# Gate logits of the last branch as seven-product block matmuls in a fp32 two-layer trunk kernel

## The chip, the cores and the metric

The kernel runs on one core of one Trainium2 chip. The metric is the device time of one execution in microseconds (us), the median of several runs. An execution under the hardware profiler gives the trace from which all rows here come; its times count from the start of its span.

The engines are TensorE (PE: matmuls and transposes, with weight loads in rows of their own, PEld), VectorE (DVE), ScalarE (ACT), GpSimd (POOL) and SyncE (SP), which issues most DMA transfers. Each engine works through its own instructions in a fixed order and waits on semaphores of the others.

## What is computed

Two layers; in each a SwiGLU FFN, a token mixer and a second FFN, each between two RMS norms and added to the residual x. x is 512 tokens by 1024.

```python
for l in range(DEPTH):
    h = rms_norm(x, norm_pre[l, 0])
    x = x + 0.5 * rms_norm(swiglu_ffn(h, ...), norm_post[l, 0])
    h = rms_norm(x, norm_pre[l, 1])
    m = hybrid_mixer(h, ...)
    x = x + rms_norm(m, norm_post[l, 1])
    ...                                   # second FFN like the first

def hybrid_mixer(h, w_in, ...):
    proj = h @ w_in                       # all inputs of the branches, and 3 x 1024 gate logits
    ...                                   # sb_out: stick-breaking attention
    ...                                   # conv_out: GLU, causal depthwise conv of 31 taps, LayerNorm, swish
    ...                                   # gla_out: gated linear attention
    branches = jnp.stack([sb_out, conv_out, gla_out], axis=2)      # each 512 wide
    branch_d = jnp.einsum('bsgw,gwd->bsgd', branches, w_branch)    # each to 1024
    gates = jax.nn.sigmoid(gate_logits.reshape(b, s, N_BRANCHES, D_MODEL))
    merged = jnp.sum(gates * branch_d, axis=2)
    return merged @ w_out
```

All of it is float32.

## The kernel before

**Products.** A float32 operand is split in two parts of a reduced float32 type: hi is a cast (ACT), lo is what is left (DVE). A product is three matmuls: hi·hi, hi·lo and lo·hi. Weights come by DMA into `raw`, are split into `whi` and `wlo` (rings of 5) and used once; `xh` and `xl` are the split, normed activations, which stay for a sub-layer.

**Gates and branches in the mixer.** The merge has 3 branches of 8 gates; a gate is 128 of the 1024 output columns. For each, PE computes the logits (`gate`, 24 matmuls of 128x512), ACT their sigmoid (`gs`), PE the branch's projection (`pb`, 12 matmuls), DVE multiplies (`gs<-pb,gs`), and POOL adds the result into `acc`. The order is attention (branch 0), gated linear attention ("GLA", branch 2), convolution (branch 1, "last"). Beside the GLA gates DVE runs the taps of the convolution and its layer norm: PE transposes `y` into `ct`, DVE makes statistics (`bs`, `mv`) and `yn`, and PE transposes `yn` back into `cb`. After the sixth GLA gate (`u_ == 5`) the last two token blocks go back; from the whole `cb` ACT makes the sigmoid `cs` and DVE the scaled `y`, then `y*cs`, then its split into `brh` and `brl`, the inputs of the last branch. PE meanwhile runs the seventh and eighth GLA gates, and then the last branch.

**Block products.** FFN tiles don't use 24 matmuls per 128 columns. `block_tiles` (L451) takes a pair of column blocks and two halves of the tokens and of the depth as a 2x2 block product with seven products in place of eight: seven times 12 matmuls of 128x256 for what plain tiling does in two times 24 of 128x512. For this it needs sums of weight blocks (`raw<-raw` on DVE), sums of token blocks `T1` to `T4` (made by the class `Forms`), and sums of the results in the PSUM banks A, B and C (copies `cp` on ACT, sums on DVE). `between(g)` is called ahead of each product g, so a caller can place other work there; weights are prepared `AHEAD` products early. The down projections (class `Down`) work with similar sums.

**What sets the order.** The instructions are written out in the order of the program text, and a scheduler at compile time fixes each engine's order from it. PE's instructions, and what is marked `pinned`, stay in program order; the rest, such as the splits of loaded weights, are placed by the scheduler. At run time each engine keeps its list. Weights are loaded through SP in the order of its list, as buffers come free.

The lines of the profile that matter: matmuls L66, transposes L71, splits L115 (ACT) and L116 (DVE), block sums, casts and wlo of `block_tiles` L455 and L457, `gs` and `acc` of the merge L1245 and L1246, the convolution's `cs`, `y` L1377 to L1379. A helper records the operations of many places, so a line can stand for several.

Of the kernel before, what the change touches and what calls it, by code (L numbers as in the profile page):

```python
# [41 lines left out]
def kernel(  # L42
# [17 lines left out]
    gp = ctx.enter_context(tc.tile_pool(name="gp", bufs=2))  # L60
    mp = ctx.enter_context(tc.tile_pool(name="mp", bufs=1))
    sm = ctx.enter_context(tc.tile_pool(name="sm", bufs=4))
    psp = ctx.enter_context(tc.tile_pool(name="psp", bufs=1, space=PSUM))

    def mm(*a, **k):
# [333 lines left out]
    class Forms:  # L399
# [7 lines left out]
        def arrive(self, i, pts):  # L407
# [11 lines left out]
            for c in range(2):  # L419
# [4 lines left out]
                for j, n in enumerate(("T3", "T4")):  # L424
                    nc.vector.tensor_tensor(self.raw[n][c][:, :, tok], t2, first[j][:, k], op=ALU.add)

        def finish(self, n):
# [20 lines left out]
    PLACES = (0, 1, 0, 2, 4, 3, 2)  # L448
    AHEAD = 6

    def block_tiles(w0, w1, fs, forms, hid, between):  # L451


        pin = pinned
        copy = lambda o, i: pin(nc.scalar.copy(o, i))  # L455
        silu = lambda o, i: pin(nc.scalar.activation(o, i, AF.Silu))
        tt = lambda o, a, b, op: pin(nc.vector.tensor_tensor(o, a, b, op=op))  # L457
        add = lambda o, a, b: tt(o, a, b, ALU.add)
        sub = lambda o, a, b: tt(o, a, b, ALU.subtract)
        n = 7 * len(fs)  # L460
        raw, banks, cps, ring = {}, {}, {}, {}

        def load(u):
            r = wp.tile([P, 5, 512], F32, tag="raw", name="raw", bufs=3)
            for w, q0 in ((w0, 0), (w1, 1)):
                for j in range(2):
                    nc.sync.dma_start(r[:, q0 + 2 * j].rearrange("p (k c) -> p k c", c=P),
                                      w[j * 512:(j + 1) * 512, fs[u] * P:(fs[u] + 1) * P]
                                      .rearrange("(k p) c -> p k c", p=P))
            raw[u] = r  # L470

        def low(g0, g1):
# [43 lines left out]

        def parts(u):
            cp = cps[u]
            return [cp[:, x * 256:(x + 1) * 256] for x in range(4)], hid[fs[u]], banks[u]

        def taken(g):

            u, j = divmod(g, 7)
            (p1, p7, u2, u4), h, (A, B, C) = parts(u)
            if j == 0:
                copy(p1, A[:, H0])
            if j == 1:
                copy(p7, C[:, H0])
            if j == 2:
                copy(u2, A[:, H0])  # L530
            if j == 4:
                copy(u4, A[:, H0])
            if j == 6:
                silu(h[:, H0], h[:, H0])
                silu(h[:, H1], A[:, H0])

        def summed(g):

            u, j = divmod(g, 7)
            (p1, p7, u2, u4), h, (A, B, C) = parts(u)  # L540
            if j == 3:
                add(h[:, H0], B[:, H0], p1)
            if j == 5:
                sub(u2, C[:, H0], u2)
                sub(u4, p7, u4)
            if j == 6:
                tt(h, cps[u][:, 512:1024], h, ALU.mult)
# [23 lines left out]
    class Down:  # L571
# [66 lines left out]
        def sums(self, p):  # L638
# [8 lines left out]
            if j >= 2:  # L647

                if self.PER == 1 and not self.apart:
                    self.apart = [gp.tile([P, D], F32, tag="g", name="kept") for n in range(2)]  # L650
# [150 lines left out]
    def ffn(wg, wu, wd, weights, forms, arrive, finish, upcoming, early, late, begin):  # L801
# [72 lines left out]
        block_tiles(wg, wu, fs, forms, hid, between)  # L874
# [4 lines left out]
    def mixer(l, wv, arrive, finish, upcoming, early, late):  # L879
# [14 lines left out]
        for i in range(NT):  # L894
# [281 lines left out]
        for h in range(HEADS):  # L1176
            ahead = att_scores(h + 1) if h + 1 < HEADS else None
            ws = att_weights(res)
            res = ahead
            if res is None:  # L1180
                for _ in fill:
                    pass
                conv_in(0)
            for _ in range(3):
                next(fill, None)
            att_values(h, ws)
        next(decay[0])
        conv_in(1)
        next(decay[0])
# [8 lines left out]

        acc = [None] * KC

        def gate_weights(g, d):
            return load_cols(W, C_GATE + g * D + d * P)

        def gate_branch(g, d, src, wb, w):
            pg = bank("gate")
            mm_cols(pg, *w)
            sg = slot("gs", tag="s")
            nc.scalar.activation(sg, pg, AF.Sigmoid)
            pb = bank("pb")
            wh, wl = wb  # L1210
# [5 lines left out]
            return pb, sg  # L1216

        def load_branch(g, d):
            wh, wl = load_cols(w_branch[l, g], d * P, 2 * P)
# [7 lines left out]
                r.append((sh, sl))  # L1227
            return r

        def gates(g, src, done):  # L1230

            early_ = done is not None
            following = gate_weights(g, 0) if early_ else None
            for d in range(0, KC, 2):
                wb = load_branch(g, d)
                for dd in (d, d + 1):
                    w = following if early_ else gate_weights(g, dd)
                    if early_ and dd + 1 < KC:
                        following = gate_weights(g, dd + 1)
                    pb, sg = gate_branch(g, dd, src, wb[dd - d], w)  # L1240
                    if acc[dd] is None:
                        acc[dd] = slot("acc", tag="q")
                        nc.vector.tensor_tensor(acc[dd], pb, sg, op=ALU.mult)
                    else:
                        nc.vector.tensor_tensor(sg, pb, sg, op=ALU.mult)  # L1245
                        nc.gpsimd.tensor_tensor(acc[dd], acc[dd], sg, op=ALU.add)  # L1246
                    if done is not None:
                        done(dd)
                    yield

        sb_gates = gates(0, branch_split(sbT, "s"), None)


        gnB = mp.tile([P, 512], F32, tag="row", name="gnB")
# [76 lines left out]
        gla_turn(*turn)  # L1331
        for _ in sb_gates:
            conv_taps(7)
        gla_gates = gates(2, branch_split(glaT, "t"), None)


        cb = []
# [44 lines left out]

        down = Down(w_out[l], acc, 0, 2, (), (4, 5, 6, 7))
        down.pairs()

        def merge(d):
            for n in range(2):
                down.sum_tokens(d, n)
            if d == KC - 2:
                for n in range(3):  # L1390
                    down.ahead()
# [23 lines left out]
    for idx, (l, s) in enumerate(subs):  # L1415
        norms = []

        def late():
            norms.append(load_g(norm_post[l, s]))
            if idx + 1 < len(subs):  # L1420
                norms.append(load_g(norm_pre[subs[idx + 1][0], subs[idx + 1][1]]))

        upcoming = []
# [58 lines left out]
```

## Time and profile before

| | |
|---|---|
| median of 3 runs | 2323.29 us (2323.27 to 2325.67) |
| profiled execution, its own time | 2321.75 us |
| its span | 2320.0 us |
| PE, DVE, ACT, POOL busy | 99%, 81%, 53%, 8% of the span |
| granted TensorE clock | 0.999 |

How to read the rows: the page's first part gives each engine's busy time, its share of the span and its count of instructions. The chain that ended last is followed back from the last instruction, and its shares say on which engine that chain lay. A row of a timeline has the start, the busy time, the engine, the line, the operation, `out<-in`, the shape and a count; in brackets stand the idle time of the engine just before it, and what ended it. Matmuls overlap in the pipeline, so the distance of two starts, not the busy time of one, is what a matmul costs. A table of stretches has one row for each stretch of time.

In layer 0 the mixer's merge lies between about 570 and 780 us, and the second layer's some 1160 us later.

### The profile page before, as it was taken

The numbers are of one execution on the slowest core, as the hardware profiler recorded it, in microseconds if no ns is written. First come the engines' busy times: TensorE is split into PE (matmuls) and PEld (weight loads), VectorE is DVE, ScalarE is ACT, GpSimd is POOL, SyncE is SP. The second block draws the span as 40 slices with busy tenths as digits, with TensorE's granted clock in tenths as the row PEclk, the third lists the DMA queues.
The fourth block names the chain that finished last, engine by engine and source line by source line (L and its number), as shares of the span: only waits on it lengthen the run. The fifth ranks groups of instructions, "written<-read, shape, count | busy, mean of one in ns | idle before, by whom it ended". The sixth has DMA issues, their size and how long they took to land.

```text
span 2320.0 us, 35537 instructions
## 1 busy us (share of the span) xinstructions
PE 2296.1 (99%) x13664; PEld 2031.0 (88%) x13664; DVE 1884.6 (81%) x2819; ACT 1240.6 (53%) x2414; POOL 177.2 (8%) x277
## 2 busy tenths in 40 slices
PE   8999999999999999999999999999999999999998
PEld 7999888887888889998889998888878888899987
DVE  7888987859965688889888889878599647888897
ACT  5555656644323565556555566566433225566664
POOL 0000001201021200000000000012010212000000
PEclk9999999999999999999999999999999999999999
DMA  5333643131333423336433336432313324333363
GB/s 174 100 101 110 229 153 102 55 103 49 110 91 106 140 73 103 99 109 235 147 87 97 108 110 235 150 88 62 97 55 105 96 91 136 91 98 104 114 222 109
DMA packets 336219, 269.49 MB, mean 116 GB/s; under 512 B 13130, under 2 KB 285548, under 8 KB 336048
## 3 DMA queue, kind: packets, MB, share of 16 engines
q1 hardware_dynamic: 336048, 267.21, 38.0%
q8 instruction: 107, 1.75, 0.3%
q14 instruction: 64, 0.52, 0.1%
HBM read 265.07 MB, written 2.10 MB: 115 GB/s over the span
## 4 chain that ended last, share of the span: by engine, by line
PE 96%; DVE 2%; ACT 1%; issue 0%; DMA 0%; POOL 0%; SPq 0%; DVEq 0%; POOLq 0%; ACTq 0%
PE A L66 19%; PE gate L66 11%; PE oA L66 10%; PE C L66 9%; PE oC L66 6%; PE pb L66 6%; PE B L66 5%; PE oB L66 3%; PE pf L66 3%; PE gr L66 2%; PE pa L66 2%; PE q L66 2%; PE gv L66 2%; PE pv L66 2%; PE pgl L66 2%; PE k L66 2%
## 5 line engine op out<-in xcount | busy, mean ns | idle before, releaser
L457 DVE TENSOR_TENSOR wlo<-raw,whi 128x1024 fp32r<-128x1024 f32 (+1 forms) x304 | 331.1, 1089 | 106.9 <-ACT whi L455 106.1
L455 ACT CAST whi<-raw 128x512 fp32r<-128x512 f32 x532 | 315.3, 620 | 164.7 <-DVE raw L457 164.7
L115 ACT CAST whi<-raw 128x1024 fp32r<-128x1024 f32 (+1 forms) x162 | 168.1, 1044 | 329.8 <-PE gate L66 143.6
L116 DVE TENSOR_TENSOR wlo<-raw,whi 128x1024 fp32r<-128x1024 f32 (+1 forms) x162 | 203.4, 1265 | 137.3 <-ACT whi L115 133.0
L457 DVE TENSOR_TENSOR raw<-raw 128x512 f32<-128x512 f32 x304 | 209.2, 688 | 5.7
L66 PE MATMUL A<-xh,whi 128*128 128x256 f32 x608 | 172.5, 284 | 0.0
L66 PE MATMUL A<-xh,wlo 128*128 128x256 f32 x608 | 172.0, 283 | 0.0
L66 PE MATMUL A<-xl,whi 128*128 128x256 f32 x608 | 172.0, 283 | 0.0
L1055 DVE SCALAR_TENSOR_TENSOR y<-u,cw,y 128x511 f32<-128x511 f32 (+14 forms) x240 | 166.7, 755 | 0.0
L686 DVE TENSOR_TENSOR wlo<-raw,whi 128x1024 fp32r<-128x1024 f32 x122 | 148.8, 1220 | 17.8 <-ACT whi L683 17.5
L683 ACT CAST whi<-raw 128x1024 fp32r<-128x1024 f32 x122 | 128.4, 1052 | 63.8 <-issue 20.8
L66 PE MATMUL gate<-xh,whi 128*128 128x512 f32 x384 | 151.3, 394 | 0.0
L66 PE MATMUL gate<-xh,wlo 128*128 128x512 f32 x384 | 149.8, 390 | 1.3 <-DVE wlo L116 1.3
L66 PE MATMUL gate<-xl,whi 128*128 128x512 f32 x384 | 149.6, 390 | 0.0
L66 PE MATMUL oA<-whi,dl 128*128 128x512 f32 x352 | 137.0, 389 | 0.0
L66 PE MATMUL oA<-whi,dh 128*128 128x512 f32 x352 | 137.0, 389 | 0.0
L66 PE MATMUL oA<-wlo,dh 128*128 128x512 f32 x352 | 136.9, 389 | 0.0
L268 POOL TENSOR_TENSOR rs<-ms,mhalf 128x1 f32<-128x1 f32 x44 | 25.1, 576 | 1415.2 <-DVE ms L266 1415.2
L455 ACT COPY cp<-A 128x256 f32<-128x256 f32 x228 | 84.4, 370 | 66.5 <-PE A L66 65.6
L66 PEld LDWEIGHTS A<-xl,whi 128*128 128x128 f32 x608 | 116.6, 192 | 0.2
L66 PEld LDWEIGHTS A<-xh,whi 128*128 128x128 f32 x608 | 116.5, 192 | 0.2
L66 PEld LDWEIGHTS A<-xh,wlo 128*128 128x128 f32 x608 | 116.5, 192 | 0.0
(330 smaller groups left out, 6947.4 us busy)
## 6 DMA issues: line engine op xcount, KB each, us to landing
raw<-in_ffn_w_down_dram SPq DMA_DIRECT2D x152, 512.0 KB, 4.5
raw<-in_w_in_dram SPq DMA_DIRECT2D x108, 512.0 KB, 4.7
raw<-in_ffn_w_gate_dram SPq DMA_DIRECT2D x168, 256.0 KB, 3.4
raw<-in_ffn_w_up_dram SPq DMA_DIRECT2D x168, 256.0 KB, 4.5
raw<-in_w_branch_dram SPq DMA_DIRECT2D x24, 512.0 KB, 4.8
raw<-in_w_out_dram SPq DMA_DIRECT2D x24, 512.0 KB, 4.9
g<-in_norm_pre_dram SPq DMA_DIRECT2D x6, 512.0 KB, 6.8
g<-in_norm_post_dram SPq DMA_DIRECT2D x6, 512.0 KB, 5.8
```

What stands on the lines that cost most here:

```text
L66: tc.keep_in_program_order(nc.tensor.matmul(*a, **k))
L115: pin(nc.scalar.copy(hi, src))
L116: pin(nc.vector.tensor_tensor(lo, src, hi.bitcast(F32), op=ALU.subtract))
L268: nc.gpsimd.tensor_tensor(self.rs, ms, mhalf[:, 0:1], op=ALU.pow)
L455: copy = lambda o, i: pin(nc.scalar.copy(o, i))
L457: tt = lambda o, a, b, op: pin(nc.vector.tensor_tensor(o, a, b, op=op))
L683: pinned(nc.scalar.copy(hi, src))
L686: pinned(nc.vector.tensor_tensor(lo, src, hi.bitcast(F32), op=ALU.subtract))
L1055: nc.vector.scalar_tensor_tensor(y[:, back:], u[:, :S - back], cw[:, c, j:j + 1], y[:, back:], op0=ALU.mult, op1=ALU.add)
```

## The change

The last branch's gate logits (branch 1, the convolution) are no longer eight times 24 matmuls of 128x512. They are made in four pairs by `block_tiles`, which takes a `source` (which columns), a `target`, a generator `result` (what is done at the end of a pair: here three sigmoids), an `ahead` (4 for this use) and a `wait`. In its `between` the mixer issues: the seventh GLA gate ahead of g = −2 and the eighth ahead of g = 0, which stood in the loop over the GLA gates; the load of the branch's weights at the third product of each pair; the branch products of the pair before, ahead of a pair's first product; the merge ahead of its second. The last pair's adds into `acc` are on DVE, the others stay on POOL.

The token sums T1 to T4 aren't there in the mixer. `Forms.rebuild` makes them from `xh` and `xl`: T1 and T2 behind the attention values of the last block (7 DVE operations and 2 casts for each half c), T3 and T4 behind the statistics of the layer norm. T1 and T2 live in the room of the residual x, which is stored to DRAM early in the mixer (`away`, four transfers of 512 KB) and loaded back during the down projection.

The convolution's layer norm begins one GLA gate earlier: the first two token blocks at `u_ == 2` (was 3), their way back and the other two at 3 (was 4). The last two still go back at `u_ == 5`.

The line numbers of after are 1 higher at the top and more further down (splits L116 and L117, `block_tiles` L492 and L493, merge L1303 and L1304, `cs` and `y` L1435 to L1437).

```diff
+        def rebuild(self, c, room_, second):
+            tt = lambda o, a, b, op: nc.vector.tensor_tensor(o, a, b, op=op)
+            def whole(hi, lo):
+                r = slot("r", tag="s").rearrange("p (k t) -> p k t", k=2)
+                tt(r, hi.bitcast(F32), lo.bitcast(F32), ALU.add)
+                return r
...
+            r11 = tokens(0, 0)
+            if not second:
+                r12 = tokens(0, 256)
+                tt(r12, r11, r12, ALU.subtract)
+                keep("T1", r12)
+                r22 = tokens(4, 256)
+                nc.vector.scalar_tensor_tensor(r22, r12, -1.0, r22, op0=ALU.mult, op1=ALU.subtract)
+                keep("T2", r22)
+                return
+            t2 = whole(*room_("T2", c))
+            tt(r11, t2, r11, ALU.add)
+            keep("T3", r11)
+            r21 = tokens(4, 0)
+            tt(r21, t2, r21, ALU.add)
+            keep("T4", r21)
...
-    def block_tiles(w0, w1, fs, forms, hid, between):
+    def block_tiles(source, count, forms, target, result, between, ahead=AHEAD, wait=0):
...
-                silu(h[:, H0], h[:, H0])
-                silu(h[:, H1], A[:, H0])
+                results[u] = result(u, h, A[:, H0], cps[u][:, 512:1024])
+                next(results[u])
...
-        for g in range(-AHEAD, n + 1):
+        for g in range(-ahead, n + 1):
             between(g)
-            f = g + AHEAD
-            if f % 7 == 0 and f < n:
-                if f == 0:
-                    load(0)
-                if f // 7 + 1 < len(fs):
-                    load(f // 7 + 1)
+            f = g + ahead
+            if f == 0:
+                load(0)
+            if f < n and (f == wait if f < 7 else f % 7 == 0) and f // 7 + 1 < count:
+                load(f // 7 + 1)
...
+        away = [scr.tile([P, D], F32, tag=f"away{i}", name=f"away{i}") for i in range(NT)]
+        for i in range(NT):
+            nc.sync.dma_start(away[i], x_sb[i])
...
             att_values(h, ws)
+        for c in range(2):
+            mforms.rebuild(c, form_room, False)
         next(decay[0])
         conv_in(1)
...
-        for u_ in range(KC):
+        for u_ in range(KC - 2):
             next(gla_gates)
-            conv_taps(10)
-            if u_ == 3:
+            conv_taps(11)
+            if u_ == 2:
                 ln_tokens(0)
                 ln_tokens(1)
-            if u_ == 4:
+            if u_ == 3:
                 ln_back(0)
                 ln_back(1)
                 ln_tokens(2)
                 ln_tokens(3)
+            if u_ in (2, 3):
+                mforms.rebuild(u_ - 2, form_room, True)
             if u_ == 5:
                 ln_back(2)
                 ln_back(3)
...
-        for _ in gates(1, cv, merge):
-            pass
-        head = down.run(late, ("B0", "B1", "C0", "C1", "D0", "D1"))
+        def sigmoids(u, h, a, second):
+            pinned(nc.scalar.activation(h[:, H0], h[:, H0], AF.Sigmoid))
+            pinned(nc.scalar.activation(h[:, H1], a, AF.Sigmoid))
+            pinned(nc.scalar.activation(second, second, AF.Sigmoid))
+            made[u].append(second)
+            yield
...
+        def merged(u):
+            if u > 0:
+                for d in (2 * u - 2, 2 * u - 1):
+                    for n in range(2):
+                        down.sum_tokens(d, n)
+            for m, (ps, sg) in enumerate(zip(pbs[u], made[u])):
+                pinned(nc.vector.tensor_tensor(sg, ps, sg, op=ALU.mult))
+                d = 2 * u + m
+                (nc.vector if u == PAIRS - 1 else nc.gpsimd).tensor_tensor(acc[d], acc[d], sg, op=ALU.add)
+
+        def between(g):
+            u, j = divmod(g, 7)
+            if g in (-2, 0):
+                next(gla_gates)
+            if 0 <= u < PAIRS and j == 2:
+                held[0] = True
+                wbs[u] = load_branch(1, 2 * u)
+                held[0] = False
+            if u > 0 and j == 0:
+                branch_products(u - 1)
+            if u > 0 and j == 1:
+                merged(u - 1)
+            if g in (7 * PAIRS - 2, 7 * PAIRS - 1, 7 * PAIRS):
+                down.ahead()
+
+        block_tiles(source, PAIRS, mforms, target, sigmoids, between, 4, 4)
+        merged(PAIRS - 1)
+
+        def back():
+            for i in range(NT):
+                if i % 2 == 0:
+                    late(i // 2)
+                x_sb[i] = resid.tile([P, D], F32, tag=f"x{i}", name=f"x{i}")
+                pinned(nc.sync.dma_start(x_sb[i], away[i]))
+
+        head = down.run(back, ("B0", "B1", "C0", "C1", "D0", "D1"))
```

How the order moves is shown at three places of layer 0. First, DVE before, around the layer norm of the last two token blocks. The first `wlo` here is that of the seventh GLA gate's weights, the second that of the eighth; the `y<-cb` operations follow right behind these rows.

```order
L116 TENSOR_TENSOR wlo<-raw,whi 128x1024
L1352 TENSOR_SCALAR yn<-ct,mv,rsc 128x512
L1348 BN_AGGR mv<-bs 128x2
L1352 TENSOR_SCALAR yn<-ct,mv,rsc 128x512
L116 TENSOR_TENSOR wlo<-raw,whi 128x1024
L1245 TENSOR_TENSOR gs<-pb,gs 128x512
L1346 BN_STATS bs<-ct 128x6 x2
L1348 BN_AGGR mv<-bs 128x2 x2
L1352 TENSOR_SCALAR yn<-ct,mv,rsc 128x512 x2
L116 TENSOR_TENSOR wlo<-raw,whi 128x1024
L1245 TENSOR_TENSOR gs<-pb,gs 128x512
L116 TENSOR_TENSOR wlo<-raw,whi 128x1024
```

Second, DVE of the change from the first `y*cs` on. L493 are operations of `block_tiles`: sums of two weight blocks and the low halves of block weights. Of the two rows `L117 ... wlo<-raw,whi 128x1024`, the one with x2 is the branch's weights and then the seventh GLA gate's; the last row is the eighth's.

```order
L1437 TENSOR_TENSOR y<-y,cs 128x512 x2
L1436 TENSOR_SCALAR y<-cb_6903,cw 128x512
L1436 TENSOR_SCALAR y<-cb_6904,cw 128x512
L1437 TENSOR_TENSOR y<-y,cs 128x512 x2
L117 TENSOR_TENSOR brl<-y,brh 128x512 x4
L493 TENSOR_TENSOR raw<-raw 128x512 x2
L493 TENSOR_TENSOR wlo<-raw,whi 128x1024
L117 TENSOR_TENSOR wlo<-raw,whi 128x1024 x2
L1303 TENSOR_TENSOR gs<-pb,gs 128x512
L493 TENSOR_TENSOR raw<-raw 128x512
L493 TENSOR_TENSOR wlo<-raw,whi 128x1024
L117 TENSOR_TENSOR wlo<-raw,whi 128x1024
```

So the two gates' low halves moved from ahead of the `yn` rows to behind `y`, `brl` and block work. On PE the seventh gate still follows the transposes into `cb`, and the eighth the seventh's branch product. ACT's order moved in the same way: `cs`, `brh`, a block's `whi`, then the branch's and the seventh gate's `whi`.

Third, SP of the change in the down projection of the mixer, with the residual's way back (`x<-away`) among the loads of `w_out` and the norm rows `g`.

```order
L128 DMA raw<-in_w_out_dram 128x2x512 x8
L128 DMA raw<-in_w_out_dram 128x1024 x2
L194 DMA g<-in_norm_post_dram 128x1024
L1502 DMA x_8005<-away_4136 128x1024
L1502 DMA x_8007<-away_4137 128x1024
L194 DMA g<-in_norm_pre_dram 128x1024
L1502 DMA x_8011<-away_4138 128x1024
L1502 DMA x_8013<-away_4139 128x1024
L128 DMA raw<-in_w_out_dram 128x1024 x2
L128 DMA raw<-in_ffn_w_gate_dram 128x2x256
```

Before, the two `g` loads stand there with one `w_out` load between them; the four loads of x are new, and the last two `w_out` loads stand behind them.

More of the change, by code (lines that the diff above doesn't have):

```diff
@@ L649, in sums @@
                 if self.PER == 1 and not self.apart:
-                    self.apart = [gp.tile([P, D], F32, tag="g", name="kept") for n in range(2)]
+                    self.apart = [gp.tile([P, D], F32, tag="g", name="kept")]
+                elif self.PER == 1 and j == 3:
+                    self.kept = room("xh", F32)
+                    self.apart.append(self.place(0))
                 if self.PER > 1:
@@ L1186, in mixer, with form_room @@
             att_values(h, ws)
+        mforms = Forms()
+        rooms = {}
+        def form_room(n, c):
+            if n not in rooms and n in ("T1", "T2"):
+                j = 0 if n == "T1" else 2
+                rooms[n] = [resid.tile([P, D], F32R, tag=f"x{j + m}", name=f"{n}{m}")
+                            .rearrange("p (k t) -> p k t", k=4) for m in range(2)]
+            if n in rooms:
+                return [r[:, 2 * c:2 * c + 2] for r in rooms[n]]
+            return [slot(n, F32R, "t" if n == "T3" else "b").rearrange("p (k t) -> p k t", k=2) for m in range(2)]
+        for c in range(2):
+            mforms.rebuild(c, form_room, False)
         next(decay[0])
@@ L1199, in mixer, with gate_branch @@
         acc = [None] * KC
[L1201 to L1206, printed above, removed]
+        def gate_branch(g, d, src, wb):
+            pg = proj_cols(W, C_GATE + g * D + d * P, "gate")
             sg = slot("gs", tag="s")
@@ L1236, in gates @@
                 for dd in (d, d + 1):
[L1237 to L1240, printed above, removed]
+                    pb, sg = gate_branch(g, dd, src, wb[dd - d])
                     if acc[dd] is None:
@@ L1384, in mixer, with source @@
         down.pairs()
[L1386 to L1391, printed above, removed]
-        for _ in gates(1, cv, merge):
-            pass
-        head = down.run(late, ("B0", "B1", "C0", "C1", "D0", "D1"))
+        PAIRS = KC // 2
+        wbs, pbs, made = {}, {}, {}
+        def source(u):
+            c0 = C_GATE + D + 2 * u * P
+            return (W, c0), (W, c0 + P)
@@ new lines, in target, with branch_products @@
+        def target(u):
+            if u not in made:
+                made[u] = [slot("gs", tag="s")]
+            return made[u][0]
+        def sigmoids(u, h, a, second):
[3 more added lines that the diff above has]
+            made[u].append(second)
+            yield
+        def branch_products(u):
+            pbs[u] = [bank("pb", "pa") for m in range(2)]
+            for ps, (wh, wl) in zip(pbs[u], wbs[u]):
+                branch_product(ps, cv, wh, wl)
@@ L1416, with late @@
         norms = []
-        def late():
-            norms.append(load_g(norm_post[l, s]))
-            if idx + 1 < len(subs):
+        def late(*which):
+            if not which or 0 in which:
+                norms.append(load_g(norm_post[l, s]))
+            if idx + 1 < len(subs) and (not which or 1 in which):
                 norms.append(load_g(norm_pre[subs[idx + 1][0], subs[idx + 1][1]]))
```

45 lines of the change are left out of this document (27 added, 18 removed).

## The prediction

> **What bounds the kernel now.** I read the page's shares and chain first, then the table of busy time in stretches, then the timelines of the engines around the end of the convolution's layer norm.
>
> ```profile
> PE 2296.1 (99%) x13664; PEld 2031.0 (88%) x13664; DVE 1884.6 (81%) x2819; ACT 1240.6 (53%) x2414; POOL 177.2 (8%) x277
> PE 96%; DVE 2%; ACT 1%; issue 0%; DMA 0%; POOL 0%; SPq 0%; DVEq 0%; POOLq 0%; ACTq 0%
> ```
>
> TensorE (PE) is busy for all but 24 of the 2320.0 us of the span, and the chain of waits runs through it. So a change can win only by giving PE less to do, and any wait that it gives PE is paid in full. The next rows are the stretches (length, then busy time and count of PE, PEld, DVE, ACT and POOL, granted clock, DMA share, GB/s):
>
> ```profile
> 640.00:680.00 40.00, 40.00 (x183) 33.19 (x182) 29.09 (x38) 10.89 (x13) 6.22 (x4) 1.00 0.38 106
> 680.00:720.00 40.00, 40.00 (x190) 33.46 (x189) 26.09 (x34) 13.75 (x19) 9.48 (x13) 1.00 0.32 87
> 720.00:760.00 40.00, 40.00 (x178) 33.10 (x178) 15.89 (x16) 9.45 (x12) 6.44 (x5) 1.00 0.30 99
> 880.00:920.00 40.00, 40.00 (x335) 40.00 (x335) 33.56 (x49) 23.38 (x52) 0.00 (x0) 1.00 0.37 107
> ```
>
> The first three are the part of the mixer that the change touches in layer 0: PE has no gap in it. The fourth is FFN2, which already runs the block products that the change brings into the mixer.
>
> **The gain.** The price of a gate and of a product is read from PE's starts:
>
> ```profile
> 730.48 0.39 PE L66 MATMUL gate<-xh,whi 128*128 128x512 f32 x1
> ...
> 735.91 0.39 PE L66 MATMUL pb<-brh,whi 128*128 128x512 f32 x1
> ...
> 860.86 0.28 PE L66 MATMUL A<-xh,whi 128*128 128x256 f32 x1
> ...
> 862.29 0.28 PE L66 MATMUL C<-T3h,whi 128*128 128x256 f32 x1
> ```
>
> A gate's 24 matmuls take 735.91 − 730.48 = 5.43 us, so a pair takes 10.86. A product's 12 matmuls take 862.29 − 860.86 = 1.43, so the seven of a pair take 10.01. The change saves 0.85 a pair. The stretches say nearly the same: 40/178 = 0.2247 us a matmul against 40/335 = 0.1194, so 48 × 0.2247 − 84 × 0.1194 = 0.76. I take 0.80, and for 4 pairs in 2 layers **6.4 us**. The branch products (pb) stay as they are.
>
> **The loss: the seventh and eighth GLA gates.** In the order of before, the low halves (wlo) of these two gates' weights stand on DVE ahead of the yn rows, and PE takes the seventh gate right behind the last transposes into cb. The trace shows the same (DVE, ACT, then PE):
>
> ```profile
> 680.10 1.26 DVE L116 TENSOR_TENSOR wlo<-raw,whi 128x1024 fp32r<-128x1024 f32 x1
> ...
> 697.22 0.69 DVE L1245 TENSOR_TENSOR gs<-pb,gs 128x512 f32<-128x512 f32 x1 [0.71 <-PE pb L66]
> 697.99 2.36 DVE L116 TENSOR_TENSOR wlo<-raw,whi 128x1024 fp32r<-128x1024 f32 x1
> 700.28 1.52 DVE L1378 TENSOR_SCALAR y<-cb,cw 128x512 f32<-128x512 f32 x2
> ...
> 705.56 0.68 DVE L116 TENSOR_TENSOR brl<-y,brh 128x512 fp32r<-128x512 f32 x1
> 706.17 1.21 DVE L116 TENSOR_TENSOR wlo<-raw,whi 128x1024 fp32r<-128x1024 f32 x1
> 707.30 1.88 DVE L116 TENSOR_TENSOR brl<-y,brh 128x512 fp32r<-128x512 f32 x3
> 709.11 0.67 DVE L1245 TENSOR_TENSOR gs<-pb,gs 128x512 f32<-128x512 f32 x1
> ```
> ```profile
> 697.87 2.79 ACT L1377 ACTIVATE cs<-cb,cw 128x512 f32<-128x512 f32 x4
> ...
> 703.29 1.05 ACT L115 CAST whi<-raw 128x1024 fp32r<-128x1024 f32 x1 [0.19 <-PE gate L66]
> ```
> ```profile
> 696.95 1.03 PE L71 MATMUL cb<-ident,yn 128*128 128x128 f32 x8
> 697.74 0.48 PE L66 MATMUL gate<-xh,whi 128*128 128x512 f32 x1
> 698.05 0.40 PE L66 MATMUL gate<-xl,whi 128*128 128x512 f32 x1
> ```
>
> The wlo at 680.10 is the seventh gate's, 17.6 us before PE starts it at 697.74, and during the y and brl work PE has two gates with their branch products (16.3 us) to run. In the changed order the seventh gate still follows the cb transposes on PE, but its wlo stands on DVE behind all eight y operations, four brl, two sums of block weights, the block's wlo and the branch's wlo; its whi on ACT stands behind cs and brh. The y work reads cb, which those very transposes complete. PE has nothing else in its queue ahead of this gate, so it idles for the whole chain:
>
> - cs of the first channel block, from 697.87 on, 0.78: with 0.13 ahead, 0.9
> - y, eight operations, 705.56 − 700.28 = 5.28
> - brl, four at (709.11 − 707.30)/3 = 0.60: 2.4
> - two block sums, and ACT's cast of the second; the block's wlo. In the FFN these are:
>
> ```profile
> L457 DVE TENSOR_TENSOR wlo<-raw,whi 128x1024 fp32r<-128x1024 f32 (+1 forms) x304 | 331.1, 1089 | 106.9 <-ACT whi L455 106.1
> L455 ACT CAST whi<-raw 128x512 fp32r<-128x512 f32 x532 | 315.3, 620 | 164.7 <-DVE raw L457 164.7
> L457 DVE TENSOR_TENSOR raw<-raw 128x512 f32<-128x512 f32 x304 | 209.2, 688 | 5.7
> ```
>
> - so 2 × 0.62 (0.69 less the overlap of about 0.07 seen between neighbours) + 0.7 + 1.1 = 3.0
> - the branch's wlo 707.30 − 706.17 = 1.13, the gate's own 1.23: 2.4
>
> Together 14.0 us. The gate's first two matmuls need only whi, ready some 10 us in, and run inside the wait (2 × 0.23): **13.5 us** lost. From below, 12, if the block's cast is early and every gap closes. From above, 16: POOL's add of the merge can fall beside a split, as at 697.99, where wlo took 2.36 against 1.21 at 706.17.
>
> The eighth gate is lost next. On DVE its wlo stands behind the seventh gate's gs, which waits for that gate's branch product, then a block sum and a wlo; on ACT its whi stands behind two casts of block weights, one on that sum. PE is free at the product's end. Then gs (697.22 − 696.95 = 0.27 to its start, 0.61 net), sum 0.6, two casts of 0.62 and 0.52 net, whi 1.05: 3.7 us to the first matmul. The wlo comes 1.2 after whi, less 0.46 of matmuls: **4.5 us**, bounds 3.5 and 6. Ahead of product 0 there is no third wait: its weights were split in the first one, and the eighth gate and its branch product give DVE 8 us.
>
> The second layer has the same order, so 2 × (13.5 + 4.5) = 36.0 us.
>
> **PE after a long idle.** PE starts the program after 7.8 us without work:
>
> ```profile
> 7.79 1.70 PE L71 MATMUL pt<-ident,hn 128*128 128x128 f32 x7
> 11.45 0.80 PE L66 MATMUL pf<-whi,xh 128*128 128x512 f32 x1 [1.96 <-ACT xh L115]
> ...
> 13.42 0.63 PE L66 MATMUL pf<-whi,xh 128*128 128x512 f32 x1
> 13.85 0.63 PE L66 MATMUL pf<-wlo,xh 128*128 128x512 f32 x1
> 14.27 0.63 PE L66 MATMUL pf<-whi,xl 128*128 128x512 f32 x1
> 14.70 0.55 PE L66 MATMUL pf<-whi,xh 128*128 128x512 f32 x1
> 15.09 0.39 PE L66 MATMUL pf<-wlo,xh 128*128 128x512 f32 x1
> ```
>
> From 13.42 to 14.70 the steps are 0.43 us, almost twice the 0.227 of a gate. Eight matmuls from 11.45 to 15.09 took 3.64 where 8 × 0.227 = 1.8 would do. So a cold PE loses up to 1.8 us. Nothing shows it cooling again in mid-program, and the granted-clock column shows 1.00 even here; bounds 0 and 1.8 for each of four waits, 0 to 7.2. I take 1.6 for each of the two long waits, which exceed the 7.8 us of the start: 3.2.
>
> [...]
>
> **What I cost at nothing, and its cover.** The first half of the rebuilt token sums adds 14 DVE operations and 4 casts per layer where DVE idles ahead of its splits:
>
> ```profile
> 499.66 1.23 DVE L116 TENSOR_TENSOR wlo<-raw,whi 128x1024 fp32r<-128x1024 f32 x1 [3.80 <-ACT whi L115]
> 505.10 1.23 DVE L116 TENSOR_TENSOR wlo<-raw,whi 128x1024 fp32r<-128x1024 f32 x1 [4.21 <-ACT whi L115]
> ```
>
> 14 × 0.61 = 8.5 us fit into gaps of some 4 us each. Without them they would be 8.5 us a layer. The second half (another 8.5) and the layer norm one gate earlier lie in the stretch 640 to 720, where DVE idles 11 to 14 us in 40. The gate after T3's casts could wait 0 to 3 us on them. In the block phase a pair of products and its branch products take 10.0 + 5.4 = 15.4 us, and on DVE stand four block sums (2.5), three and a half wlo (3.8), the branch's wlo (1.1), two gs (1.2) and, my estimate, 3 us of bank and token sums: 11.6 us, a share of 75%. The last pair's adds go to DVE, and the first down product can wait 0 to 1.3 us on them.
>
> The residual x is stored to DRAM and read back, 2 MB each way per layer. The stores go out early in the mixer, far from any peak. The loads stand between the w_out loads on SP:
>
> ```profile
> 775.00:780.00 5.00, 5.00 (x24) 4.14 (x23) 5.00 (x9) 2.34 (x5) 0.00 (x0) 1.00 0.69 229
> 780.00:785.00 5.00, 5.00 (x24) 4.14 (x23) 5.00 (x8) 3.14 (x5) 2.56 (x1) 1.00 0.98 351
> 785.00:800.00 15.00, 15.00 (x68) 12.43 (x67) 13.68 (x20) 13.41 (x23) 6.74 (x1) 1.00 0.66 223
> ```
>
> At 351 GB/s 2 MB are 6.0 us, which the w_out weights split ahead cover; at half that rate 12, of which some 9 would reach the down projection. I take 0, bounds 0 and 10 a layer.
>
> **The sum.** 36.0 + 3.2 − 6.4 = +32.8. Against the profiled execution's 2321.75 us (span 2320.0) that is 2354.6. That execution lies 1.5 below the median of the runs, 2323.29, so the forecast is **2356 us**.
>
> **Rivals.**
> 1. The waits are as above, and PE cools in the shorter ones too: 4 × 1.8 = 7.2 in place of 3.2, 2360. For it: the half rate at the start. Against: the start has no history, so the rows don't show what cools PE. [...]
> 2. The read-back collides with w_out in the down projection: 9 us a layer, 2374. For it: a DMA share of 0.98 already at 780. Against: the share was 0.69 just before, and 0.66 just after.
> 3. The block phase becomes DVE's: with POOL's adds beside it, each pair runs 1 us late, 8 pairs, 2364. For it: the POOL add at 782.44 below took 9.29 beside a full DVE, 1.29 with DVE half idle. Against: FFN2 holds PE at 40.00 of 40 with DVE at 33.56.
>
> ```profile
> 697.99 1.29 POOL L1246 TENSOR_TENSOR acc<-acc,gs 128x512 f32<-128x512 f32 x1 [6.15 <-DVE gs L1245]
> 782.44 9.29 POOL L1246 TENSOR_TENSOR acc<-acc,gs 128x512 f32<-128x512 f32 x1 [8.73 <-DVE gs L1245]
> ```
>
> 4. The other side: no wait at all. PE reaches the seventh gate so late that its weights are split, because the second half of the sums and the earlier layer norm hold up the y work's release and PE alike; only the gain is left: 2323.3 − 6.4 = 2317. It decides if PE is at least 13.5 us behind DVE there. Against it: the chain begins with the PE transposes themselves, so a later PE only moves it.
> 5. The waits shrink to half, if the chain overlaps more than the order tells (brl and block sums finished beside y): 18 + 1.6 − 6.4 = +13, 2336.
>
> **Chances.** Forecast 0.52, rivals 0.12, 0.14, 0.10, 0.07 and 0.05 in turn. A measurement of this kernel tells changes of over 0.2% (4.6 us) from none. Faster is rival 4: 0.07. Within 0.2% would need the waits to shrink to about the gain, from the tail of rival 5: 0.03. Slower is the rest, 0.90. The forecast's own range is 12 + 3.5 to 16 + 6 a layer with the cold PE: 2348 to 2368. The range to hold 8 in 10 takes in most of rivals 1 to 3: **2342 to 2376**.
>
> **What would show it.** In the table of PE's waits of the changed kernel, the gate waiting for the wlo and whi of L117, two long waits of about 10 us (to whi) with 3 to 4 more to wlo, and two of 4 to 5. PE's busy time in matmuls falls by about 6 us. After the long waits some 8 matmuls step at 0.43. The block products of the mixer take 0.119 a matmul. If PE shows no gap behind the cb transposes, the central step is wrong; if oC or oA wait for DMA in the down projection, rival 2 was right; if A, B or C wait for copies or wlo of L493 pair after pair, rival 3.

## The result

The changed kernel takes 2363.98 us (median of 4, 2362.70 to 2364.29) against 2323.93 before (2323.27 to 2325.67). The ratio is 1.0172 with a 95% interval of 1.016 to 1.0184: slower by 40 us, where 33 were forecast.

The page of the changed kernel, first its busy times, and from the table of PE's waits the total, the count and the longest of each kind:

```profile
PE 2304.9 (98%) x13952; PEld 2044.7 (87%) x13952; DVE 1952.8 (83%) x2951; ACT 1274.7 (54%) x2510; POOL 157.9 (7%) x273
...
PE gate L67 <- ACT whi L116: 25.4, 4, 9.1
PE gate L67 <- DVE wlo L117: 9.8, 6, 3.6
```

The span is 2362.5 us, 42.5 longer than the one before. Before, PE waited 1.3 us for a gate's wlo and never for its whi; now it waits 35.2 for both. That is 33.9 more. The rest stands in PE's busy time, which grew by 8.8, from 2296.1 to 2304.9, although the block products should have taken 6.4 from it. So PE also ran slowly somewhere. The stretches show where:

```profile
680.00:720.00 40.00, 27.30 (x121) 22.09 (x120) 21.96 (x33) 10.86 (x17) 5.42 (x7) 0.83 0.10 27
720.00:760.00 40.00, 35.71 (x209) 31.44 (x208) 18.71 (x24) 14.34 (x28) 6.27 (x4) 0.91 0.18 53
```

Where PE had been busy for all of 680 to 760, it now has gaps of 17 us, and beside them the granted clock (the third number from the right) falls to 0.83 and 0.91. PE's timeline of that place, with the idle time and its end in brackets:

```profile
697.63 1.03 PE L72 MATMUL cb<-ident,yn 128*128 128x128 f32 x8
707.79 0.80 PE L67 MATMUL gate<-xh,whi 128*128 128x512 f32 x1 [9.13 <-ACT whi L116]
...
712.59 0.80 PE L67 MATMUL gate<-xh,wlo 128*128 128x512 f32 x1 [3.58 <-DVE wlo L117]
713.18 0.63 PE L67 MATMUL gate<-xh,whi 128*128 128x512 f32 x1
...
716.16 0.47 PE L67 MATMUL gate<-xl,whi 128*128 128x512 f32 x1
...
725.88 0.50 PE L67 MATMUL gate<-xh,whi 128*128 128x512 f32 x1 [3.57 <-ACT whi L116]
726.21 0.40 PE L67 MATMUL gate<-xl,whi 128*128 128x512 f32 x1
727.33 0.80 PE L67 MATMUL gate<-xh,wlo 128*128 128x512 f32 x1 [0.72 <-DVE wlo L117]
...
733.04 0.55 PE L67 MATMUL gate<-xh,whi 128*128 128x512 f32 x1
...
738.01 0.28 PE L67 MATMUL A<-xh,whi 128*128 128x256 f32 x1
```

The four waits stand where the prediction put them: behind the transposes into cb, first for the seventh gate's whi, then its wlo, and again for both of the eighth gate. Behind each pair of waits the matmuls step by 0.43 us (712.59 to 716.16, and 727.33 to 733.04) and then by 0.23. DVE and ACT at the same time:

```profile
699.24 1.53 DVE L1436 TENSOR_SCALAR y<-cb,cw 128x512 f32<-128x512 f32 x2 [0.66 <-ACT cs L1435]
...
704.53 2.49 DVE L117 TENSOR_TENSOR brl<-y,brh 128x512 fp32r<-128x512 f32 x4
706.94 1.41 DVE L493 TENSOR_TENSOR raw<-raw 128x512 f32<-128x512 f32 x2
709.04 1.22 DVE L493 TENSOR_TENSOR wlo<-raw,whi 128x1024 fp32r<-128x1024 f32 x1 [0.69 <-ACT whi L492]
710.18 2.35 DVE L117 TENSOR_TENSOR wlo<-raw,whi 128x1024 fp32r<-128x1024 f32 x2
722.42 0.69 DVE L1303 TENSOR_TENSOR gs<-pb,gs 128x512 f32<-128x512 f32 x1 [9.88 <-PE pb L67]
```
```profile
698.43 2.78 ACT L1435 ACTIVATE cs<-cb,cw 128x512 f32<-128x512 f32 x4 [2.67 <-PE cb L72]
...
704.10 1.22 ACT L116 CAST brh<-y 128x512 fp32r<-128x512 f32 x2 [1.42 <-DVE y L1437]
...
705.75 1.99 ACT L116 CAST whi<-raw 128x1024 fp32r<-128x1024 f32 x2
...
724.79 1.04 ACT L116 CAST whi<-raw 128x1024 fp32r<-128x1024 f32 x1
```

From 699.24 on DVE works through y, brl, block sums and block weights with 0.69 us of idle time, and comes to the seventh gate's wlo last (the second of the two at 710.18). Then it idles for 9.88 us at `gs`, with the eighth gate's split behind it in its list. ACT casts the branch's whi and the seventh gate's behind `cs` and `brh` (705.75, done at 707.74, when PE's first wait ends) and the eighth gate's only at 724.79, done when PE's third wait ends. The weights themselves were not late. SP had issued the last load of this group by 671 us, and the next one followed at 712.6:

```profile
670.46 0.58 SPq L128 DMA_DIRECT2D raw<-in_w_branch_dram  x1
712.60 32.39 SPq L503 DMA_DIRECT2D raw<-in_w_in_dram  x8
```

### The profile page after: what moved, and what is told of

Read it like the earlier page. It is cut to its first block, busy times and chain, and to the rows that moved or that the text cites. A ratio compares the mean times of both kernels' runs of the same rounds, so it can differ in the third digit from the quotient of the medians.

```text
span 2362.5 us, 36365 instructions
## 1 busy us (share of the span) xinstructions
PE 2304.9 (98%) x13952; PEld 2044.7 (87%) x13952; DVE 1952.8 (83%) x2951; ACT 1274.7 (54%) x2510; POOL 157.9 (7%) x273
## 5 line engine op out<-in xcount | busy, mean ns | idle before, releaser
L493 DVE TENSOR_TENSOR wlo<-raw,whi 128x1024 fp32r<-128x1024 f32 (+1 forms) x336 | 365.9, 1089 | 126.5 <-ACT whi L492 125.6
L492 ACT CAST whi<-raw 128x512 fp32r<-128x512 f32 x588 | 349.1, 620 | 189.1 <-DVE raw L493 186.0
L116 ACT CAST whi<-raw 128x1024 fp32r<-128x1024 f32 (+2 forms) x146 | 151.0, 1042 | 199.8 <-PE gate L67 63.0
L493 DVE TENSOR_TENSOR raw<-raw 128x512 f32<-128x512 f32 x336 | 232.3, 691 | 5.9
L117 DVE TENSOR_TENSOR wlo<-raw,whi 128x1024 fp32r<-128x1024 f32 (+2 forms) x146 | 174.3, 1207 | 61.2 <-ACT whi L116 55.5
L67 PE MATMUL A<-xh,whi 128*128 128x256 f32 x672 | 190.6, 284 | 0.0
L67 PE MATMUL A<-xh,wlo 128*128 128x256 f32 x672 | 190.1, 283 | 0.0
L492 ACT COPY cp<-A 128x256 f32<-128x256 f32 x252 | 93.2, 370 | 102.4 <-PE A L67 101.6
L67 PE MATMUL gate<-xh,whi 128*128 128x512 f32 x256 | 105.6, 412 | 25.4 <-ACT whi L116 25.4
L67 PE MATMUL gate<-xh,wlo 128*128 128x512 f32 x256 | 104.3, 407 | 9.8 <-DVE wlo L117 9.8
L67 PE MATMUL gate<-xl,whi 128*128 128x512 f32 x256 | 103.1, 403 | 0.0
```

Of the source, the lines that this page charges most:

```text
L67: tc.keep_in_program_order(nc.tensor.matmul(*a, **k))
L116: pin(nc.scalar.copy(hi, src))
L117: pin(nc.vector.tensor_tensor(lo, src, hi.bitcast(F32), op=ALU.subtract))
```

## The experiments

In each, the kernel before ran on the same chip, at 2324.0 us in the first four and 2323.8 in the second four.

**1. Splits ahead.** The weights of the last two GLA gates and their branch are loaded and split ahead of the last transposes.

```diff
...
             if u_ == 5:
+                ready["b", 2, 6] = load_branch(2, 6)
+                ready[2, 6] = load_cols(W, C_GATE + 2 * D + 6 * P)
+                ready[2, 7] = load_cols(W, C_GATE + 2 * D + 7 * P)
                 ln_back(2)
                 ln_back(3)
```

A gate or a branch product whose weights are in `ready` takes them from there in place of loading them.

> The changed kernel with one edit: the weights of the seventh and eighth GLA gates, and of their branch, are loaded and split in the program text ahead of the last transposes into cb. PE's order is not changed. Theory (PE waits for these splits, and runs cold behind each wait): the four waits a layer go, 33.9 us in all with some 14 of slow matmuls; what is left is the block gain of 6.4 and a new wait of about 2.3 us a layer at the sixth gate, whose buffers now come free later. 2318 to 2324 us. Rival (the block phase or the added DVE and DMA work costs the time itself, and the waits only show it): the time stays at 2340 or more, with waits of A, B, C or oA in place of those of gate.

Measured: 2321.94 us, ratio to before 0.9990 (0.9981 to 0.9999). The waits for whi and wlo are gone, all but the 1.3 us of old, and the new one is there, smaller than expected:

```profile
PE gate L67 <- ACT gs L1276: 2.6, 2, 1.3
PE gate L67 <- DVE wlo L117: 1.3, 2, 0.6
```

From these three early loads and splits, with PE's order as it was, came 42 us. The block products, the rebuilt sums and the transfers of x are all still in this kernel, so none of them was the loss.

**2. Splits ahead and the sums one gate later.** In addition the second half of T3 and T4 moves away from the sigmoid that the wait above ends on.

```diff
-            if u_ in (2, 3):
-                mforms.rebuild(u_ - 2, form_room, True)
+            if u_ in (2, 4):
+                mforms.rebuild(u_ // 2 - 1, form_room, True)
```

> Like the one before, and in addition the second half of T3 and T4 is rebuilt one gate later (at the gates 2 and 4 in place of 2 and 3), so that the fifth gate's sigmoid doesn't stand behind its casts on ACT. Theory: no wait is left in the stage, the full gain of 0.8 a pair remains, 6.4 us: 2317.5 us against 2324 before, and PE is busy for all of 640 to 780. Rival (the added DVE, DMA and POOL work is not hidden after all): within 2 us of 2324, or slower.

Measured: 2318.53 us (7 runs), ratio 0.9974 (0.9963 to 0.9984): faster than both kernels by 5.5 us against the one before, where 6.4 were expected. PE's stretches have no gap, and a clock of 1.00:

```profile
680.00:720.00 40.00, 40.00 (x209) 34.31 (x207) 30.49 (x43) 16.18 (x28) 10.09 (x9) 1.00 0.10 27
720.00:760.00 40.00, 40.00 (x275) 37.32 (x274) 27.32 (x40) 18.57 (x38) 5.93 (x4) 1.00 0.44 132
760.00:800.00 40.00, 40.00 (x216) 34.35 (x215) 36.44 (x53) 27.91 (x49) 3.00 (x2) 1.00 0.70 244
...
697.16 1.03 PE L72 MATMUL cb<-ident,yn 128*128 128x128 f32 x8
...
714.37 0.28 PE L67 MATMUL A<-xh,whi 128*128 128x256 f32 x1
```

From the last transposes into cb to the first block product PE takes 714.37 − 697.16 = 17.21 us here; in the changed kernel 738.01 − 697.63 = 40.38. So layer 0 lost 23.2 us at this one place. By the same two rows layer 1 took 17.21 here and 39.51 in the change, a loss of 22.3.

**3. The two gates back in the loop.**

```diff
-        for u_ in range(KC - 2):
+        for u_ in range(KC):
...
-            if g in (-2, 0):
-                next(gla_gates)
```

> The changed kernel with the seventh and eighth GLA gates issued in the loop over the GLA gates, as before, and not out of the block tiles. Theory: their splits go ahead again, and what is late next is the first block product's wlo, with the two gates and branch products as its cover: waits of about 2.3 us at the sixth gate, 4 at product 0 and 0.5 in A, a layer; with the 6.4 of gain 2331 us, up to 2337 if the 4 us wait cools PE. Rival (the place of the gates doesn't matter, the wait is the y work's): 2355 or more.

Measured: 2336.00 us, ratio 1.0049 (1.0035 to 1.0063). As expected the wait moved on to the first block product. Behind it the matmuls of 128x256 step at 0.21 us (0.12 from 728.35 on), and the granted clock over 5 us is 0.62:

```profile
PE A L67 <- DVE wlo L493: 9.6, 2, 4.8
...
720.00:725.00 5.00, 2.32 (x11) 2.32 (x12) 3.08 (x4) 2.23 (x4) 0.17 (x1) 0.62 0.00 0
```

The last two gates cover the y work, as before, but the block weights then have no cover. Of the 40 us lost, 28 come back. So issuing these gates from inside the block tiles was not the fault by itself: run 1 leaves them there and loses nothing. What the changed kernel lacked were the early splits.

**4. PE kept busy in the waits.** Idle matmuls into an unused bank stand ahead of the last two gates; nothing reads them.

```diff
+            if g == 2 and d in (6, 7):
+                pw = bank("warm")
+                for _ in range(56 if d == 6 else 19):
+                    mm(pw, cur["xh"][:, 0, 0:P], cur["xh"][:, 1, :], start=True, stop=True)
             pg = proj_cols(W, C_GATE + g * D + d * P, "gate")
```

> The changed kernel with idle work for PE: 56 matmuls of 128x512 into an unused bank ahead of the seventh gate, and 19 ahead of the eighth; their result is not used. They take 12.7 and 4.3 us at full rate and end about when the weights come. Theory (PE runs at half rate after a long wait, some 7 us lost a layer): the waits in the trace all but vanish, the end of each does not move, and the gates run at 0.227 a matmul: 2364 less 10 to 14, 2350 to 2354 us. Rival (the rate has another cause, such as contention with DVE's splits): 2364 us, with steps of 0.43 still there.

Measured: 2357.36 us (2356.57 to 2358.15), 6.6 below the changed kernel, at a clock of 1.000. The size was missed, the sign was right, and the trace says why:

```profile
699.39 1.03 PE L72 MATMUL cb<-ident,yn 128*128 128x128 f32 x8
700.18 12.95 PE L67 MATMUL warm<-xh 128*128 128x512 f32 x56
714.37 0.50 PE L67 MATMUL gate<-xh,wlo 128*128 128x512 f32 x1 [0.78 <-DVE wlo L117]
...
722.21 4.47 PE L67 MATMUL warm<-xh 128*128 128x512 f32 x19
727.39 0.50 PE L67 MATMUL gate<-xh,wlo 128*128 128x512 f32 x1 [0.26 <-DVE wlo L117]
...
735.23 0.28 PE L67 MATMUL A<-xh,whi 128*128 128x256 f32 x1
```

The first wait ends at the same distance from the transposes (14.98 us against 14.96 in the change), since DVE sets it. From there to product 0 PE takes 735.23 − 714.37 = 20.86 us in place of 738.01 − 712.59 = 25.42. That is 4.6 us; layer 1 gains 3.7 by the same rows. The expectation of 10 to 14 was too high. Without its 17.0 us of waits, the change takes 40.38 − 17.0 = 23.4 us from cb to product 0 in layer 0 where run 2 takes 17.2, and 22.5 in layer 1, so PE's busy time there is 11.5 longer in all. But 3.3 of it lie inside the waits, mostly in the matmuls between the two waits of a gate, and those cost nothing, because PE would have waited anyway. The two layers give 8.2 us; the runs gave 6.6. In the profiled execution some 1.8 us were lost in the first FFN's down projection, where the kernels don't differ; a part of the 1.6 may lie there.

**5. The fault alone, in the kernel before.** No block, no rebuilt sum, no transfer; the splits of the two gates are held behind y and brl by keeping these in program order.

```diff
         for u_ in range(KC):
+            held[0] = u_ > 5
             next(gla_gates)
+            held[0] = False
...
-                    nc.vector.tensor_scalar(ys[c], cb[c], g_, b_, op0=ALU.mult, op1=ALU.add)
-                    nc.vector.tensor_tensor(ys[c], ys[c], s_, op=ALU.mult)
+                    pinned(nc.vector.tensor_scalar(ys[c], cb[c], g_, b_, op0=ALU.mult, op1=ALU.add))
+                    pinned(nc.vector.tensor_tensor(ys[c], ys[c], s_, op=ALU.mult))
+                held[0] = True
                 cv = branch_split(ys, "s")
+                held[0] = False
```

> The kernel before with one thing of the change alone: the y and brl work and the splits of the seventh and eighth GLA gates' weights are kept in program order, so these splits stand behind y and brl on DVE and ACT. No block product, no rebuilt sum, no transfer of x. Theory: PE waits 9.2 + 1.6 us ahead of the seventh gate and 1.7 ahead of the eighth, 12.5 a layer, and runs cold after the long wait for 2 to 4.7 us: 2324 plus 28 to 35, 2352 to 2359. Rival (the waits need the blocks, since only there DVE and the weight buffers are short): 2324 to 2330.

Measured: 2352.12 us, ratio 1.0123 (1.0108 to 1.0138), 28 us from order alone:

```profile
PE gate L66 <- ACT whi L115: 18.1, 2, 9.1
...
PE gate L66 <- DVE wlo L116: 6.0, 6, 1.5
```

18.1 + 6.0 − 1.3 = 22.8 us of waits, and the matmuls behind the long wait step at 0.43 here too. The waits are somewhat shorter than in the change, since no block work stands between brl and these splits.

**6. The seventh gate's splits ahead, the eighth's not.** The edit of run 1 without its third line.

> The changed kernel with the weights of the branch and of the seventh GLA gate alone split ahead; the eighth's are left where they are. Theory: no wait at the seventh gate; the y work and the block weights now fall beside that gate, so the eighth waits longer than in the change, 7 us for whi and 1 for wlo in place of 3.6 and 0.7; with 2.8 of cold matmuls behind it and the gain: 2324 - 6.4 + 2 x 11.2 = 2340. Rival (the eighth's wait only follows from the seventh's): 2320.

Measured: 2339.44 us, ratio 1.0069 (1.0054 to 1.0084).

```profile
PE gate L67 <- ACT whi L116: 14.2, 2, 7.1
```

The eighth's wait isn't a mere consequence of the seventh's. Without the seventh's, its wait for whi doubles (7.1 us in place of 3.57), as forecast from y and brl falling beside the seventh gate.

**7. PE kept busy ahead of the eighth gate alone.** The edit of run 4 with `d == 7` and the 19 matmuls only.

> The changed kernel with idle work for PE ahead of the eighth gate alone, 19 matmuls of 128x512. In the run with both fills 1.9 us a layer were won behind the first wait and 2.8 behind the second, from the starts of the matmuls. Theory (each wait cools PE by itself, even one of 3.6 us): 2364 - 2 x 2.8 = 2358. Rival (PE is still cold from the first wait when the second comes): nothing to win here, 2363 or more.

Measured: 2360.62 us (2358.70 to 2363.12), 3.4 below the changed kernel and halfway between the two expectations. The intervals of the two kernels' ratios to before overlap (1.0140 to 1.0174 here, 1.0160 to 1.0184 for the change), so the trace has to decide. From cb to product 0 it has

```profile
699.57 1.03 PE L72 MATMUL cb<-ident,yn 128*128 128x128 f32 x8
...
737.77 0.28 PE L67 MATMUL A<-xh,whi 128*128 128x256 f32 x1
```

38.20 us against 40.38, 2.2 less; in layer 1 it is 1.7 less. So the eighth gate's waits do cool PE by themselves, even though its steps had been back at 0.23 us for 5.5 us before them (716.47 to 721.92 in the change), and each of the two gates costs some 2 us a layer in this way.

**8. x read back twice.** Run 2 with every load of x issued twice.

```diff
-                pinned(nc.sync.dma_start(x_sb[i], away[i]))
+                for again in range(2):
+                    pinned(nc.sync.dma_start(x_sb[i], away[i]))
```

> The run with splits and sums moved (2318.5 us), with each of the four loads of x in the down projection issued twice: 2 MB more for each layer. Theory (the read-back is hidden with little to spare): each 2 MB take 6 us of a full DMA, and a part shows as waits for w_out or for FFN2's first weights: 2319 to 2325 us. Rival (DMA has room to spare): 2318.5. If the first 2 MB already cost, then waits of oA, oC or pf on weights would show in both, at 2325 or more here.

Measured: 2328.42 us (2326.86 to 2332.23), 9.9 above run 2 and more than expected. The down projection and the next FFN's first weights now wait:

```profile
PE oC L67 <- ACT whi L720: 2.3, 1, 2.3
...
PE oC L67 <- DVE wlo L723: 1.2, 2, 0.8
```

With 1.0 and 0.8 for whi and wlo of pf these are 5.3 us of waits, and slow matmuls stand behind some of them. In run 2, with one read-back, none of these rows exists, though the DMA share there reaches 0.99:

```profile
785.00:795.00 10.00, 10.00 (x46) 8.29 (x45) 10.00 (x16) 9.78 (x17) 0.00 (x0) 1.00 0.99 367
```

So the first 2 MB are hidden, with less than another 2 MB to spare.

## Why the prediction was right, and what it missed

**The central step held.** PE's order was unchanged at the seventh gate, DVE's and ACT's were not, and PE idled for the whole chain. Forecast were 13.5 and 4.5 us a layer. From the first cb row to the first wlo matmul of the seventh gate the trace has 712.59 − 697.63 = 14.96; less 0.79 for the transposes and 0.46 for the two matmuls inside it is 13.7. By its parts, from the starts of DVE: 5.29 for y (forecast 5.28), 2.41 for brl (2.4), 3.24 for the block sums and the block's wlo (3.0), 2.35 for the two wlo at the end (2.4). For the eighth gate run 4 takes from 722.21, the end of the branch product, to 727.39, which is 5.2 us, as the change does; less 0.46, 4.7. Together 18.4 a layer against 18.0.

**The mis-sized term is the cold PE.** The prediction took 1.6 us for each of the two long waits, 3.2 in all, and nothing for the waits of the eighth gate; rival 1, with 7.2, had a chance of 0.12. By the starts in run 4 against the change it is 4.6 and 3.7 us in the two layers, 8.2 in all. The step that failed is "I take 1.6 for each of the two long waits": the eighth gate's shorter waits cool PE as well and cost 2.2 and 1.7 us (run 7), and what is left for the long ones is 4.3, some 2.1 each. So rival 1 was right on this term, and even a little short, and the bounds of 0 to 7.2 did not hold it. A slip at the start of the program is a part of that: from 11.45 to 15.09 there are seven steps, not eight matmuls, so the cold start loses 3.64 − 7 × 0.227 = 2.05 us (with 0.15 of a wait in it) and not 1.8.

**The sum as measured.** 2 × 18.4 of waits and 8.2 of cold matmuls make 45.0 of the 45.5 us that the stretch from cb to product 0 lost in the two layers against run 2. The gain can be read from starts too, up to the first product of the down projection (oA), here before, in run 2 and in the change:

```profile
782.15 0.39 PE L66 MATMUL oA<-whi,dh 128*128 128x512 f32 x1
...
779.25 0.39 PE L67 MATMUL oA<-whi,dh 128*128 128x512 f32 x1
...
802.89 0.39 PE L67 MATMUL oA<-whi,dh 128*128 128x512 f32 x1
```

From the last transposes into cb (696.95, 697.16 and 697.63) these are 85.20, 82.09 and 105.26 us; in layer 1 they are 85.21, 82.09 and 104.39. So the block products win 3.1 us a layer, 6.2 in all where 6.4 were forecast, and the change loses 20.1 and 19.2 there: 39.2 of the 40.05 us by which the medians differ. The other 0.8 us is not traced to a place. The forecast of 2356 missed the time by 8 us; 5.0 of them are the cold matmuls, 0.8 the waits and 0.2 the gain, and the rest are differences of under 1 us each. The range held it.

**What was costed at nothing** cost next to nothing. In run 2 all of it is in the kernel, and PE has no new wait. The exception is the second half of the sums: the prediction allowed 0 to 3 us there and took 0. In the change the wait doesn't show; with the splits ahead it is 1.3 us a layer (run 1). No slow steps follow it; run 2 wins 3.4 us in all by moving the sums, and the 0.8 beyond the two waits are not traced.

**The other rivals.** Rival 2, the collision in the down projection, did not happen; run 8 shows that it begins within the next 2 MB a layer. Rival 3, a block phase bound by DVE: in run 2 PE is busy for 40.00 of 40 there with DVE at 27.32, and still at the end of the phase with DVE at 36.44, so no. Rival 4, no wait at all, fell with the first table of waits; its time, 2317, is nearly what run 2 reached (2318.53), when the splits really stood ahead. Rival 5, half the waits: the chain did not overlap more than the order told, since DVE idled for 0.69 us in it.

## What to carry to other kernels

When work is moved to another place of the program, look at what else that place issues: the gates' matmuls kept their place on PE, and their splits, two instructions a gate on two other engines, went 14 us back. The loss can be summed from the order and from durations of the old trace, to 0.4 us in 18 here; the cure was to issue the small preparations early and leave the large work where it was. And waits of PE cost more than their length here: behind each gate's waits the matmuls at 0.43 us in place of 0.227 cost some 2 us more, while the 3.3 us in all that slow matmuls took longer inside the waits cost nothing. No length came out below which a wait is safe from this: 1.3 us (run 1) and 1.5 (run 5) were, 2.3 (run 8) was not, and two of 0.96 and 0.76 close together (run 8) were not either.

## What the runs showed of the hardware that was not expected

**PE slows after short waits, in mid-program.** Waits of 9.1 (the change), 7.1 (run 6) and 4.8 us (run 3) were each followed at once by steps of 0.43 us for a matmul of 128x512 (0.21 for 128x256), in the middle of full work. Behind the eighth gate's wait of 3.57 us in the change it was not at once: the first step is 0.33 us (725.88 to 726.21), as behind the wait of 1.31 in run 1 (691.00 to 691.33), and the slow steps begin behind the next wait, of 0.72. That wait in run 1 and one of 1.5 us in run 5 had no slow steps behind them: after the first, of 0.33 and 0.34, they are 0.22 to 0.24. But the length of one wait does not decide alone. In run 8 steps of 0.43 stand behind one of 2.32 us in layer 1, and in layer 0 behind two of 0.96 and 0.76 us close together:

```profile
1955.03 0.80 PE L67 MATMUL oC<-whi,dh 128*128 128x512 f32 x1 [2.32 <-ACT whi L720]
...
823.19 0.50 PE L67 MATMUL pf<-whi,xh 128*128 128x512 f32 x1 [0.96 <-ACT whi L116]
824.45 0.50 PE L67 MATMUL pf<-wlo,xh 128*128 128x512 f32 x1 [0.76 <-DVE wlo L117]
...
825.06 0.63 PE L67 MATMUL pf<-whi,xh 128*128 128x512 f32 x1
825.49 0.63 PE L67 MATMUL pf<-wlo,xh 128*128 128x512 f32 x1
```

What does decide is open. The granted clock was 0.83 over the 40 us from 680 on; over 5 us of them it was 0.50:

```profile
710.00:715.00 5.00, 2.41 (x6) 1.95 (x7) 2.53 (x3) 0.00 (x0) 0.00 (x0) 0.50 0.24 61
```

This stretch of the changed kernel takes in the seventh gate's second wait. At the start of the program before, with the same slow steps of 0.43 us (13.42 to 14.70), the column read 1.00, so it can't be relied on there:

```profile
12.00:15.00 3.00, 2.85 (x7) 1.79 (x6) 2.55 (x6) 3.00 (x7) 0.56 (x1) 1.00 1.07 391
```

**The slow time varies.** Behind the seventh gate's waits the slow steps lasted 3.6 us in layer 0 (712.59 to 716.16) and 4.4 in layer 1 (1885.75 to 1890.19), behind the eighth's 5.7 (727.33 to 733.04) and 3.2 (1900.96 to 1904.11). Why is open.
